# The rows of gate maxima and stabilisers, spread over the partitions by products or by reads from DRAM

## The chip, the cores and the metric

The kernel runs on one core of a Trainium2 chip. The metric is the device time of one execution in microseconds (us). The core has a matrix engine (TensorE, PE, with its weight loads as PEld), a vector engine (VectorE, DVE), an engine for functions (ScalarE, ACT), a general engine (GpSimd, POOL), and a sequencer for transfers (SyncE, SP). Working memory is SBUF with 128 partitions; PE writes its results to PSUM, which is divided into eight banks of 128 x 512 floats. Inputs, outputs and the `sums` tiles lie in DRAM; sixteen DMA engines carry the transfers between DRAM and SBUF.

## The reference

One layer of a hybrid encoder block at 512 positions and width 1024: RMSNorm, one input projection into 10240 columns, a Fourier branch, an mLSTM branch with four heads of width 512, sigmoid gates that merge the two, an output projection, a residual and a final norm. The change touches the gates of the mLSTM branch only. Per head and direction:

```
bcum = jnp.cumsum(ft, axis=-1)
dmat = bcum[..., :, None] - bcum[..., None, :] + it[..., None, :]
m_t = jnp.maximum(bcum + m_st[..., None], jnp.max(dmat, axis=-1))
s_mat = jnp.einsum('bhtd,bhsd->bhts', qt, kt) * jnp.exp(dmat - m_t[..., None])
...
h_out = num / jnp.maximum(jnp.abs(den), jnp.exp(-m_t))[..., None]
```

`ft` is the logarithm of the forget gate, `it` the input gate. The kernel computes this for all 512 positions at once instead of chunk by chunk. With `a = it - bcum` and `mx` the running maximum of `a`, the weight of source position s for target t is exp(a[s] - mx[t]), and the stabiliser is m[t] = bcum[t] + mx[t]. The weights are held as tiles with s in the partitions and t along the row; so `a` is needed as a column (one value per partition), but `mx` and `m` are needed as rows that stand in all partitions.

## The kernel before

All large products run in single-precision `float32r` form, split in two: a high part (`hi_of`, an ACT copy to `float32r`) and a low part (`lo_of`, a DVE subtraction), and three products per pair (`mm3`). Weights come as units of 512 KB (`fetch`, SP, into three buffers named `raw`); `prepare` splits a unit into `whi`/`wlo` (two buffers) and issues the next fetch; `unit` hands out a split unit and keeps the next one ready. At certain counts `unit`, and twice per head the head's own code, call `next_job`: SP copies a 1 MB weight block from DRAM to DRAM (`sum`, L159) and POOL's queue adds another block onto an earlier one (L163). These sums are used much later, behind the four heads.

The order is partly written by hand. The framework's planner orders the instructions of each engine with a timing model when the program is built; what it chose is then fixed, and each engine issues in that order. `pin` ties an instruction to its place behind the one before it on the same engine or queue. All of the kernel's transfers that SP issues in the heads are pinned, so SP keeps the order of the program, and an instruction on SP that waits holds all those behind it.

Ahead of the heads lie the projections of the conv channels, the convolution, the product that gives the gates (`gate_mm`, L302), and two z units. Then four heads run (`for h in range(NH)`, L474). In a head:

- q is projected (`mm3` at L498); in head 0 `gate_chain` (L420) follows, which makes the rows for all heads and both directions at once: biased gates (L433, L434), log-sigmoid, scans on DVE (L443, L447), and copies that put the backward rows into forward order (L451, L452). The results are `an` (for `a`), `mxn` (for `mx`) and `mn` (for `m`), 64 x 512 tiles; row 32 dr + h belongs to direction dr and head h. `gate_cols` (L459) transposes `an` to columns `a_col`.
- `mx_r` and `em_r` (L453 to L455) hold the rows of `mxn` and `mn` as high parts in partitions 0 to 63 and low parts in 64 to 127. `bsel` (L456) holds selector columns.
- `decay` (L512): per direction one product (L516) with a selector column as stationary side puts row h of `mx` into all partitions of a PSUM bank; eight exponentials (L521) read it and write the weight tiles `wf`; POOL clears the triangles (L525, L528).
- The products q k (L539, banks `sps`) are multiplied with the weights on DVE (L576, L577), summed over source blocks (L589 to L593), split (L605, L606) and summed over partitions by products with `half_r` (L608) into `den`: partitions 0 to 63 hold the forward sum, the others the backward sum.
- One product (L602) with `bw` (L601), made from `bsel`, puts `m` of the forward direction into partitions 0 to 63 of the bank `bc` and that of the backward direction into the others. `em` = exp(-bc) (L610); then the maximum with |den|, the reciprocal (L613, L614), and the scaling of the weights (L623 to L625), their split, the products v (L636), and the products with v (L651).
- The o products (`o_part`, L557 to L559) and z units are put between these steps as work for PE. In head 0 the last z unit runs ahead of `gate_cols` and `decay`; o units 0 and 1 and three pieces of unit 2 stand ahead of L608.

Of the kernel before, what the change touches and what calls it, by code (L numbers as in the profile page):

```python
# [40 lines left out]
def hybrid_block(ctx: ExitStack, tc, xT, xn, first, units, blocks, vecs, gates, gbias, consts, dft, fnw, out):  # L41
# [23 lines left out]
    def tl(tag, shape, dtype=F32, bufs=1, pool=None, shift=0):  # L65
        count[0] += 1
        if pool is None:
            pool = "wide" if tag[:2] in ("sa", "sb") else "gw" if tag in ("gwh", "gwl") else "low" if tag in LOW else "high" if tag in HIGH else "work"


        n = math.prod(shape[1:])
        t = pools[pool][1].tile([shape[0], -(-(n + shift) // 64) * 64], dtype, tag=tag, name=f"{tag}_{count[0]}", bufs=bufs)
        t = t[:, shift : shift + n]
        if len(shape) == 2:
            return t
        names = "abcd"[: len(shape) - 1]
        return t.rearrange(f"p ({' '.join(names)}) -> p {' '.join(names)}", **dict(zip(names, shape[1:])))
# [8 lines left out]
    def pin(ins, on=True):  # L86
        return tc.keep_in_program_order(ins) if on else ins
# [325 lines left out]
            gate_mm(pending[::-1])  # L413

    a_col = tl("a_col", [P, 4, 64])
    em_r = tl("em_r", [P, S], F32R)
    mx_r = tl("mx_r", [P, S], F32R)
    bsel = tl("bsel", [P, 8], F32R)

    def gate_chain():  # L420

        gb = tl("gb", [64, 2])
        pin(nc.sync.dma_start(gb, gbias))
        graw = t2k()
        se.activation(graw, gate_ps, AF.Copy)
        spare = [tl(t, [64, 2, S]) for t in ("so0", "so1")]
        s0, s1, s2, s3 = spare[0][:, 0, :], spare[0][:, 1, :], spare[1][:, 0, :], spare[1][:, 1, :]
        s4, s5 = tl("wf2", [64, S]), tl("wf3", [64, S])
        ig, z, e, u, w = s0, s1, s2, s3, s4
        for j, t in enumerate((ig, z)):  # L430
            sp = bank("acc", rows=64)
            te.matmul(sp, ident_c[:, C_SEL + 64 * j : C_SEL + 64 * j + 64], graw, start=True, stop=True)
            se.activation(t[0:32, :], sp[0:32, :], AF.Identity, bias=gb[0:32, j : j + 1])  # L433
            se.activation(t[32:64, ::-1], sp[32:64, :], AF.Identity, bias=gb[32:64, j : j + 1])  # L434
        se.activation(e, z, AF.Abs)
        se.activation(e, e, AF.Exp, scale=-1.0)
        ve.tensor_scalar(out=u, in0=e, scalar1=1.0, scalar2=None, op0=ALU.add)
        ve.scalar_tensor_tensor(out=w, in0=u, scalar=-1.0, in1=e, op0=ALU.add, op1=ALU.subtract)
        se.activation(u, u, AF.Ln)
        ve.scalar_tensor_tensor(out=w, in0=z, scalar=0.0, in1=w, op0=ALU.min, op1=ALU.add)  # L440
        ve.tensor_tensor(out=w, in0=w, in1=u, op=ALU.subtract)
        fc = e
        ve.tensor_tensor_scan(out=fc, data0=ones[0:64, 0:1].to_broadcast([64, S]), data1=w, initial=0.0,  # L443
                              op0=ALU.mult, op1=ALU.add)
        a, mx = u, z
        ve.tensor_tensor(out=a, in0=ig, in1=fc, op=ALU.subtract)
        ve.tensor_tensor_scan(out=mx, data0=a, data1=a, initial=0.0, op0=ALU.max, op1=ALU.max)  # L447
        ve.tensor_tensor(out=fc, in0=fc, in1=mx, op=ALU.add)
        an, mxn, mn = s5, s0, s4
        for dst, srct in ((an, a), (mxn, mx), (mn, fc)):  # L450
            ve.tensor_copy(dst[0:32, :], srct[0:32, :])  # L451
            ve.tensor_copy(dst[32:64, ::-1], srct[32:64, :])  # L452
        for dst, srct in ((mx_r, mxn), (em_r, mn)):  # L453
            se.activation(dst[0:64, :], srct, AF.Copy)
            ve.tensor_tensor(out=dst[64:128, :], in0=srct, in1=dst[0:64, :].bitcast(F32), op=ALU.subtract)  # L455
        pin(se.activation(bsel, ident_c[:, C_BSEL : C_BSEL + 8], AF.Copy))  # L456
        return an

    def gate_cols(an):  # L459
# [14 lines left out]
    for h in range(NH):  # L474
# [37 lines left out]
        def decay():  # L512
            ws = [tl(f"wf{b}", [P, 640]) for b in range(4)]
            for dr in range(2):
                bc = bank("acc")
                te.matmul(bc, bsel[:, 4 * dr + h : 4 * dr + h + 1].to_broadcast([P, P]), mx_r, start=True, stop=True)  # L516
                for b in range(4):
                    n = (b + 1) * P
                    o, s = (slice(n, 640), slice(b * P, S)) if dr == 0 else (slice(0, n), slice(0, n))
                    r = 32 * dr + h  # L520
                    se.activation(ws[b][:, o], bc[:, s], AF.Exp, scale=-1.0, bias=a_col[:, b, r : r + 1])  # L521
            for b in range(4):
                n = (b + 1) * P
                blk = ws[b][:, n : n + P]
                gp.affine_select(out=blk, in_=blk, compare_op=ALU.is_ge, fill=0.0, base=0,  # L525
                                 pattern=[[1, P]], channel_multiplier=-1)
                blk = ws[b][:, n - P : n]
                gp.affine_select(out=blk, in_=blk, compare_op=ALU.is_ge, fill=0.0, base=0,  # L528
                                 pattern=[[-1, P]], channel_multiplier=1)
            return ws  # L530
# [64 lines left out]
        early = 3 if h == 0 else 0  # L595
        w2 = unit()
        o_part(2, w2, PIECES[:early])
        em, bc, den = tl("phi2", [P, S]), bank("wk"), bank("wk")
        halves = [slice(0, 64), slice(64, 128)]
        bw = tl("plo2", [P, 2, 64], F32R)  # L600
        se.activation(bw, bsel.bitcast(F32).rearrange("p (r i) -> p r i", r=2)[:, :, h : h + 1].to_broadcast([P, 2, 64]), AF.Copy)  # L601
        te.matmul(bc, bw.rearrange("p r m -> p (r m)"), em_r, start=True, stop=True)  # L602
        for dr, acc in enumerate((sf, sb_)):
            sh, sl = tl(f"vhi{3 - dr}", [P, S], F32R), tl(f"vlo{3 - dr}", [P, S], F32R)
            hi_of(sh, acc)  # L605
# [1 line left out]
            for part, rr in enumerate((sh, sl)):  # L607
                te.matmul(den, half_r[:, dr, :], rr,  # L608
                          start=dr == 0 and part == 0, stop=dr == 1 and part == 1)
        se.activation(em, bc, AF.Exp, scale=-1.0)  # L610
        r = t2k()
        se.activation(r, den, AF.Abs)
        ve.tensor_tensor(out=r, in0=r, in1=em, op=ALU.max)  # L613
# [45 lines left out]
        for d in range(4):  # L659
            if h > 0 and d > 0:  # L660
                z_unit(d)
            c = c0 + d
            se.activation(xc[c], xc[c], AF.Copy, scale=col(V_SK + c))
        for d in range(4):
            c = c0 + d
            tp = bank("wk")
            for t in range(4):
                te.transpose(tp[:, t * P : (t + 1) * P], so[t][:, d * P : (d + 1) * P], ident)  # L668
            uu = t2k()
            ve.scalar_tensor_tensor(out=uu, in0=tp, scalar=col(V_HN + c), in1=xc[c], op0=ALU.mult, op1=ALU.add)  # L670
            ve.tensor_tensor(out=uu, in0=uu, in1=sz[d], op=ALU.mult)
            u_hi[c] = tl(f"sa{c}", [P, S], F32R)
            u_lo[c] = tl(f"sb{c}", [P, S], F32R)
            hi_of(u_hi[c], uu)
            lo_of(u_lo[c], uu, u_hi[c])
# [482 lines left out]
```

## Time and profile before

| | |
|---|---|
| median of three runs | 758.74 us (758.71 to 758.91) |
| the profiled execution | 758.77 us |
| its span in the trace | 756.8 us |
| mean granted clock of PE | 0.997 |
| PE busy | 747.5 us, 4134 products |
| DVE, ACT, POOL busy | 526.7, 411.8, 69.7 us |
| moved by DMA | 128.55 MB, 170 GB/s mean |

The profiled execution's own time is two microseconds above the span, which runs from the first to the last instruction of the program. Rows of a timeline give start and length in us, the engine, the line of the kernel, the operation, what it writes and reads, and shapes; a bracket at the end tells how long the engine sat idle before it and for whom. "SPq" rows are transfers issued by SP; their length is the issue, and the transfers themselves land later. In rows of the DMA view the last number is the median time from issue to landing. A product's length includes its way through the array; the next product starts before it ends.

### The profile page before, as it was taken

The page shows a single profiled execution, that of the slowest core. Times are in us where ns is not written, and L with a number is a line of the kernel's source. Part 1 is how long each engine was busy: PE and PEld are TensorE (multiplying, and loading weights), DVE is VectorE, ACT ScalarE, POOL GpSimd, SP SyncE. Part 2 cuts the span into 40 slices and gives each one's busy share as a digit, 9 for nine tenths or more (in the row PEclk, how much of TensorE's full clock was granted, in tenths as well). Part 3 has the DMA queues.
Part 4 walks back from the last instruction along what each step waited for, and adds up shares of the span by engine and source line. Part 5 has one row for each costly group of instructions (what it writes and reads, how often), then busy time and mean ns, then how long its engine had stood idle before and what let it go on. Part 6 is the DMA issues. An engine that isn't in the chain of part 4 may idle for free.

```text
span 756.8 us, 10920 instructions
## 1 busy us (share of the span) xinstructions
PE 747.5 (99%) x4134; PEld 642.3 (85%) x4134; DVE 526.7 (70%) x821; ACT 411.8 (54%) x645; POOL 69.7 (9%) x147
## 2 busy tenths in 40 slices
PE   9999999999999999999999999999999999999996
PEld 7888876888888888888888888899999999988885
DVE  6999983696658575867493856257676687556976
ACT  7336466478547663776372443266544587543444
POOL 0000000104100310041003010000020100000003
PEclk9999999999999999999999999999999999999998
DMA  8548775276924892479215873377655456554452
GB/s 301 168 141 227 209 256 141 48 244 150 225 101 156 212 241 69 162 180 228 100 59 166 221 228 106 88 216 213 190 162 163 114 163 197 171 182 153 139 195 111
DMA packets 40805, 128.55 MB, mean 170 GB/s; under 512 B 4785, under 2 KB 5426, under 8 KB 35634
## 3 DMA queue, kind: packets, MB, share of 16 engines
q1 hardware_dynamic: 36802, 104.41, 41.4%
q0 software_dynamic: 3520, 23.07, 15.3%
q8 instruction: 32, 0.52, 0.3%
q10 hardware_dynamic: 432, 0.40, 0.2%
q14 instruction: 19, 0.16, 0.1%
HBM read 125.76 MB, written 44.04 MB: 224 GB/s over the span
## 4 chain that ended last, share of the span: by engine, by line
PE 96%; DVE 1%; ACT 1%; DMA 0%; POOL 0%; issue 0%; POOLq 0%; ACTq 0%
PE acc L97 17%; PE acc L99 17%; PE acc L98 17%; PE wk L97 8%; PE wk L99 8%; PE wk L98 8%; PE acc L558 3%; PE acc L557 3%; PE acc L559 3%; PE wk L636 2%; PE acc L1006 1%; PE acc L1008 1%; PE acc L1007 1%; PE wk L302 1%; PE wk L668 1%; PE wk L608 1%
## 5 line engine op out<-in xcount | busy, mean ns | idle before, releaser
L93 DVE TENSOR_TENSOR wlo<-raw,whi 128x1024 fp32r<-128x1024 f32 (+2 forms) x107 | 124.9, 1171 | 79.0 <-ACT whi L90 78.6
L90 ACT ACTIVATE whi<-raw 128x1024 fp32r<-128x1024 f32 (+2 forms) x107 | 108.6, 1019 | 126.3 <-PE acc L98 76.5
L97 PE MATMUL acc<-hhi,whi 128*128 128x512 f32 x240 | 94.3, 393 | 0.6 <-ACT whi L90 0.6
L98 PE MATMUL acc<-hlo,whi 128*128 128x512 f32 x240 | 93.6, 390 | 0.0
L99 PE MATMUL acc<-hhi,wlo 128*128 128x512 f32 x240 | 93.5, 390 | 0.0
L93 DVE TENSOR_TENSOR gwl<-raw,gwh 128x1024 fp32r<-128x1024 f32 (+1 forms) x39 | 47.1, 1208 | 16.9 <-ACT gwh L90 16.9
L90 ACT ACTIVATE gwh<-raw 128x1024 fp32r<-128x1024 f32 (+1 forms) x39 | 40.9, 1048 | 29.0 <-PE acc L98 10.0
L97 PEld LDWEIGHTS acc<-hhi,whi 128*128 128x128 f32 x240 | 45.1, 188 | 11.1 <-ACT whi L90 1.2
L99 PEld LDWEIGHTS acc<-hhi,wlo 128*128 128x128 f32 x240 | 45.0, 188 | 9.5
L98 PEld LDWEIGHTS acc<-hlo,whi 128*128 128x128 f32 x240 | 45.1, 188 | 9.1
L559 PE MATMUL acc<-whi,hlo 128*128 128x512 f32 x128 | 50.4, 394 | 0.0
L558 PE MATMUL acc<-wlo,hhi 128*128 128x512 f32 x128 | 50.4, 394 | 0.0
L98 PE MATMUL acc<-sb,whi 128*128 128x512 f32 x128 | 50.1, 391 | 0.0
L97 PE MATMUL acc<-sa,whi 128*128 128x512 f32 x128 | 49.8, 389 | 0.0
L98 PE MATMUL wk<-vlo,phi 128*128 128x512 f32 x128 | 49.8, 389 | 0.0
L97 PE MATMUL wk<-vhi,phi 128*128 128x512 f32 x128 | 49.6, 389 | 0.0
L99 PE MATMUL acc<-sa,wlo 128*128 128x512 f32 x128 | 49.0, 391 | 0.0
L99 PE MATMUL wk<-vhi,plo 128*128 128x512 f32 x128 | 48.0, 389 | 0.0
L557 PE MATMUL acc<-whi,hhi 128*128 128x512 f32 x128 | 47.7, 393 | 0.0
L331 DVE SCALAR_TENSOR_TENSOR t2k<-sa,vecs,t2k 128x511 f32<-128x511 f32 (+1 forms) x64 | 45.1, 743 | 0.1
L93 DVE TENSOR_TENSOR vlo<-wk,vhi 128x512 fp32r<-128x512 f32 x32 | 20.6, 676 | 15.7 <-ACT vhi L90 15.7
L98 PEld LDWEIGHTS acc<-sb,whi 128*128 128x128 f32 x128 | 24.0, 188 | 5.0
(409 smaller groups left out, 1910.8 us busy)
## 6 DMA issues: line engine op xcount, KB each, us to landing
raw<-in_units_dram SPq DMA_DIRECT2D x69, 512.0 KB, 4.2
sum<-in_blocks_dram SPq DMA_DIRECT2D x20, 1024.0 KB, 8.0
raw<-sum SPq DMA_DIRECT2D x64, 256.0 KB, 3.6
raw<-in_blocks_dram SPq DMA_DIRECT2D x48, 256.0 KB, 3.8
sum<-in_blocks_dram POOLq DMA_DIRECT2D x10, 1024.0 KB, 10.6
sum<-sum POOLq DMA_DIRECT2D x10, 1024.0 KB, 8.6
raw<-sum SPq DMA_DIRECT2D x8, 512.0 KB, 4.2
raw<-in_blocks_dram SPq DMA_DIRECT2D x6, 512.0 KB, 4.1
```

Of the source, the lines that this page charges most:

```text
L90: pin(se.activation(dst, src, AF.Copy, scale=scale), pinned)
L93: pin(ve.tensor_tensor(out=dst, in0=src, in1=hi.bitcast(F32), op=ALU.subtract), pinned)
L97: pin(te.matmul(acc, wh, xh, start=start, stop=False, **skip), pinned)
L98: te.matmul(acc, wh, xl, start=False, stop=False, **skip)
L99: te.matmul(acc, wl, xh, start=False, stop=stop, **skip)
L302: pin(te.matmul(gate_ps[rows, :], w_gate[j][:, i, :], r, start=n == 0, stop=n == 14, tile_position=(0, 32 * (2 * b + j))), n + b + j > 0)
L331: ve.scalar_tensor_tensor(out=cv[:, o], in0=src[:, s], scalar=cw[k], in1=cv[:, o], op0=ALU.mult, op1=ALU.add)
L557: te.matmul(ops[t], hv(x_hi, k)[:, ts], wh[:, ks], start=k == 0, stop=False)
L558: te.matmul(ops[t], hv(x_hi, k)[:, ts], wl[:, ks], start=False, stop=False)
L559: te.matmul(ops[t], hv(x_lo, k)[:, ts], wh[:, ks], start=False, stop=k == 7)
L608: te.matmul(den, half_r[:, dr, :], rr, start=dr == 0 and part == 0, stop=dr == 1 and part == 1)
L636: te.matmul(vp[:, ds], xm[c0 + d][:, b * P : (b + 1) * P], vbf[:, d, :], start=True, stop=True)
```

## The change

The products that spread rows (L516 and L602) and what feeds them (`mx_r`, `em_r` as split tiles, `bsel`, `bw`) go. `mxn` and `mn` are written to two DRAM tiles of 64 x 512 (`rows0`, `rows1`) by SP, and `spread_rows(h)` reads them back for one head: row 32 dr + h of `mx` into all 128 partitions, once per direction (256 KB each), and the two rows of `m` into 64 partitions each of one tile `em` (128 KB each). The tiles have one buffer, so a read waits until the head before has used them. The reads for head 0 are issued at the end of the gate chain, those for head h + 1 near the end of head h, after its z units; all are pinned, as are both writes. The copies to forward order are put in another order: `mxn` first, then `an`, then `mn`. The exponentials then read SBUF, and `em` is computed in place.

```diff
+    kept_rows = [dram.tile([64, S], F32, tag=f"rows{j}", name=f"rows{j}") for j in range(2)]
+    spread = {}
+
+    def spread_rows(h):
+        for dr in range(2):
+            r = 32 * dr + h
+            spread[dr] = tl(("mx_r", "em_r")[dr], [P, S])
+            pin(nc.sync.dma_start(spread[dr], kept_rows[0][r : r + 1, :].to_broadcast([P, S])))
+        spread[2] = tl("em", [P, S])
+        for dr in range(2):
+            r = 32 * dr + h
+            pin(nc.sync.dma_start(spread[2][64 * dr : 64 * dr + 64], kept_rows[1][r : r + 1, :].to_broadcast([64, S])))
...
-        for dst, srct in ((an, a), (mxn, mx), (mn, fc)):
-            ve.tensor_copy(dst[0:32, :], srct[0:32, :])
+        for n, (dst, srct) in enumerate(((mxn, mx), (an, a), (mn, fc))):
+            pin(ve.tensor_copy(dst[0:32, :], srct[0:32, :]), n > 0)
             ve.tensor_copy(dst[32:64, ::-1], srct[32:64, :])
-        for dst, srct in ((mx_r, mxn), (em_r, mn)):
-            se.activation(dst[0:64, :], srct, AF.Copy)
-            ve.tensor_tensor(out=dst[64:128, :], in0=srct, in1=dst[0:64, :].bitcast(F32), op=ALU.subtract)
-        pin(se.activation(bsel, ident_c[:, C_BSEL : C_BSEL + 8], AF.Copy))
+            if n != 1:
+                pin(nc.sync.dma_start(kept_rows[n // 2], dst))
+        spread_rows(0)
         return an
...
             for dr in range(2):
-                bc = bank("acc")
-                te.matmul(bc, bsel[:, 4 * dr + h : 4 * dr + h + 1].to_broadcast([P, P]), mx_r, start=True, stop=True)
+                bc = spread[dr]
...
-        em, bc, den = tl("phi2", [P, S]), bank("wk"), bank("wk")
+        em, den = spread[2], bank("wk")
         halves = [slice(0, 64), slice(64, 128)]
-        bw = tl("plo2", [P, 2, 64], F32R)
-        se.activation(bw, bsel.bitcast(F32).rearrange("p (r i) -> p r i", r=2)[:, :, h : h + 1].to_broadcast([P, 2, 64]), AF.Copy)
-        te.matmul(bc, bw.rearrange("p r m -> p (r m)"), em_r, start=True, stop=True)
...
-        se.activation(em, bc, AF.Exp, scale=-1.0)
+        se.activation(em, em, AF.Exp, scale=-1.0)
...
+        if h < NH - 1:
+            spread_rows(h + 1)
         for d in range(4):
             c = c0 + d
             tp = bank("wk")
```

More of the change, by code (lines that the diff above doesn't have):

```diff
@@ L415, in hybrid_block @@
     a_col = tl("a_col", [P, 4, 64])
-    em_r = tl("em_r", [P, S], F32R)
-    mx_r = tl("mx_r", [P, S], F32R)
-    bsel = tl("bsel", [P, 8], F32R)
+    kept_rows = [dram.tile([64, S], F32, tag=f"rows{j}", name=f"rows{j}") for j in range(2)]
[9 more added lines that the diff above has]
+            pin(nc.sync.dma_start(spread[2][64 * dr : 64 * dr + 64], kept_rows[1][r : r + 1, :].to_broadcast([64, S])))
     def gate_chain():
```

## The prediction

> **What bounds the kernel.** I read the page first (busy shares, then the chain that ended last), next the waits of TensorE (PE), then PE's timeline around the products that the change removes, and last the timelines of ACT, DVE and SyncE (SP) around the gate chain of head 0. Of the page:
>
> ```profile
> span 756.8 us, 10920 instructions
> ...
> PE 747.5 (99%) x4134; PEld 642.3 (85%) x4134; DVE 526.7 (70%) x821; ACT 411.8 (54%) x645; POOL 69.7 (9%) x147
> ...
> GB/s 301 168 141 227 209 256 141 48 244 150 225 101 156 212 241 69 162 180 228 100 59 166 221 228 106 88 216 213 190 162 163 114 163 197 171 182 153 139 195 111
> ...
> PE 96%; DVE 1%; ACT 1%; DMA 0%; POOL 0%; issue 0%; POOLq 0%; ACTq 0%
> ```
>
> PE is busy 747.5 of 756.8 us and holds 96% of the chain. "Busy" alone could hide gaps, since products overlap; so I also read PE's waits (who was waited for, total us, times, longest):
>
> ```profile
> PE wk L196 <- POOL mhalf L183: 1.1, 1, 1.1
> PE acc L97 <- ACT whi L90: 0.6, 1, 0.6
> PE wk L608 <- ACT vhi L90: 0.4, 1, 0.4
> ```
>
> Three waits, 2.1 us in all, 1.1 of them at the very start. So PE sets the time nearly everywhere, and a product taken away is worth the distance from its start to the start of the next one, if no new wait takes its place. These distances stand in PE's timeline (start, us, engine, line); the last two rows are pieces of the chain of waits:
>
> ```profile
> 140.24 0.74 PE L516 MATMUL acc<-mx_r,bsel 128*128 128x512 f32 x2
> 140.81 0.40 PE L557 MATMUL acc<-whi,hhi 128*128 128x512 f32 x1
> ...
> 151.72 0.39 PE L602 MATMUL wk<-em_r,plo 128*128 128x512 f32 x1
> 152.55 0.50 PE L608 MATMUL wk<-vhi,half_r 128*128 128x512 f32 x1 [0.45 <-ACT vhi L90]
> 152.89 1.72 PE L636 MATMUL wk<-mhi,sa 128*128 128x128 f32 x14
> ...
> 169.03 0.40 PE L516 MATMUL acc<-mx_r,bsel 128*128 128x512 f32 x1
> 169.26 0.39 PE L97 MATMUL wk<-vhi,phi 128*128 128x512 f32 x1
> ...
> 169.88 0.49 PE L516 MATMUL acc<-mx_r,bsel 128*128 128x512 f32 x1
> 170.22 0.40 PE L97 MATMUL wk<-vhi,phi 128*128 128x512 f32 x1
> ...
> 221.03 0.39 PE L602 MATMUL wk<-em_r,plo 128*128 128x512 f32 x1
> 221.26 0.39 PE L97 MATMUL acc<-hhi,whi 128*128 128x512 f32 x1
> ...
> 238.68 0.47 PE acc L516 x2
> ...
> 313.87 0.47 PE acc L516 x2
> ```
>
> The duration column (0.39) is not the price: the next product starts 0.23 us later.
>
> **What it removes from PE.** Twelve products: per head two at L516 and one at L602. Pairs of L516: head 0 0.57 (140.24 to 140.81), head 1 0.23 + 0.34, heads 2 and 3 0.47 each: 2.08 us. L602: 0.23 in each of four heads (221.03 to 221.26; in head 0 the rest of its 0.83 is the wait of L608): 0.92 us. Sum 3.0 us.
>
> **What of it is real time.** Heads 1 to 3 hold 2.2 us of it, with PE gapless before and after: real. In head 0 it is 0.57 + 0.23 = 0.80, and there PE already waits for ACT at L608. That chain runs from the last z product over ACT's exponentials and DVE's products to L608, and the removed products are not on it; so PE would only come 0.8 us sooner to the same wait. What can fill it is L636: 14 of these products (the v of this head) run right behind L608 at 152.89, and they need neither removed operand. One PSUM bank (`bc` at L598) also becomes free for them. The planner issues what is ready, so I take them as moved ahead: the 0.8 is real, and the 0.45 of wait may go too. If not, head 0 gives nothing.
>
> **What it takes from ACT and DVE.**
>
> ```profile
> 136.03 0.63 ACT L454 ACTIVATE mx_r<-so 64x512 fp32r<-64x512 f32 x1 [6.21 <-DVE so L452]
> ...
> 137.67 0.31 ACT L601 ACTIVATE plo<-bsel 128x128 fp32r<-128x128 f32 x1
> ...
> 144.05 3.46 ACT L521 ACTIVATE wf<-acc,a_col 128x512 f32<-128x512 f32 x8
> ...
> 152.93 1.04 ACT L90 ACTIVATE whi<-raw 128x1024 fp32r<-128x1024 f32 x1
> ```
>
> ```profile
> 132.56 1.22 DVE L447 TENSOR_TENSOR_SCAN so<-so 64x512 f32<-64x512 f32 x1
> ...
> 135.58 0.42 DVE L452 COPY so<-so 32x512 f32<-32x512 f32 x1
> ...
> 136.91 0.69 DVE L455 TENSOR_TENSOR mx_r<-so,mx_r 64x512 fp32r<-64x512 f32 x1
> ```
>
> ACT loses two L454 (0.63 each), four L601 (0.31 each) and a tiny one at L456, some 2.7 us; DVE two L455, 1.4 us. Both engines have idle time (54% and 70% busy) and their results come well before PE needs them; I count zero. The exponentials now read SBUF instead of PSUM: the trace has ACT copies of 128x512 from both sides at about the same length, so zero again, bounded by PE's slack on both sides.
>
> **What it adds: the round trip in head 0.** The maxima are written to DRAM when their copies are done. Before, that is 135.58 + 0.42 = 136.0; the change puts these copies first, so up to 1.4 us sooner (the scan ends at 133.8). I keep 136.0. No row shows a write of gate rows or a read of one row into all partitions, so bounds come from the nearest DMAs (last number: median us to landing):
>
> ```profile
> yb<-in_xn_dram SPq DMA_DIRECT2D x8, 256.0 KB, 2.6
> out_dram<-yb SPq DMA_DIRECT2D x7, 256.0 KB, 2.3
> ...
> vlo<-in_xT_dram SPq DMA_DIRECT2D x4, 256.0 KB, 6.0
> ...
> gb<-in_gbias_dram SPq DMA_DIRECT2D x1, 0.5 KB, 7.3
> ```
>
> The write is like `out_dram<-yb` (SBUF to DRAM, 2.3; half its bytes), each read like `yb<-in_xn` (128 rows of 2 KB, 2.6); high, both like `vlo<-in_xT`, 6.0, which stood in a full queue. Near case: 136.0 + 2.3 + 2.6 = 140.9, the second read some 0.6 behind (SP's issue), 141.5. The exponentials start at 144.05, after a table load that follows the last z unit's SiLU: 2.5 us of cover, cost zero. High case: 136.0 + 6.0 + 6.0 = 148.0, 4 us late.
>
> The Trainium skill, page "DMA: Bandwidth & Descriptors", section "Latency and other measured facts", speaks against this read: it reports that partition streams running in step at a large power-of-two row pitch fall to about 103 GB/s, and guesses that they hit the same HBM channel. A read of one row by all partitions has pitch zero, so it may be the extreme of that; by 103 GB/s (an estimate from that page) a read takes about 2.5 us of transfer, the second would land near 145, the first near 143. By it the sum stays as it is and only the cover shrinks (the second direction's exponentials start half-way through L521's 3.46 us). No row of before shows such a read.
>
> **What it adds: SP's queue.** SP issues in the order of the program. The write stands behind `gb` and ahead of a block copy and the next fetches:
>
> ```profile
> 104.18 0.59 SPq L423 DMA_DIRECT2D gb<-in_gbias_dram  x1
> 104.81 0.65 SPq L159 DMA_DIRECT2D sum<-in_blocks_dram  x1
> ...
> 108.77 5.58 SPq L131 DMA_DIRECT2D raw<-in_units_dram  x2
> 114.41 0.50 SPq L159 DMA_DIRECT2D sum<-in_blocks_dram  x1
> ...
> 156.39 0.33 SPq L131 DMA_DIRECT2D raw<-in_units_dram  x1
> ...
> 237.43 0.33 SPq L131 DMA_DIRECT2D raw<-in_units_dram  x1
> ...
> 312.08 0.33 SPq L131 DMA_DIRECT2D raw<-in_units_dram  x1
> ```
>
> So a copy of 1 MB, two weight fetches and one more copy, issued at 104.8 to 114.4, wait behind SP's instruction until the maxima are written (about 138.3), then behind the four reads, to about 141. This is a large shift, 27 to 32 us, and its cover must be named: the two fetches (units for o products 2 and 3) are split by ACT only from 152.93 on. Ahead of the first lie 0.75 MB of reads, 1 MB of copy and its own 0.5 MB: at 250 to 300 GB/s (the page's busy slices) 7.5 to 9 us from 138.3, so 146 to 147.5; the second 2 us later. Five and four us of cover; cost zero. If one came after 152.93, PE would wait for it one to one. The copies feed block sums used after 400 us; POOL's add behind the first copy is issued behind head 0's masks, so it holds nobody.
>
> **Heads 1 to 3.** The reads are issued behind the fetches at 156.39, 237.43 and 312.08. L521 of head 1 cannot start before 169.03, 12 us later. For head 2 and 3:
>
> ```profile
> 243.49 2.62 ACT L521 ACTIVATE wf<-acc,a_col 128x512 f32<-128x512 f32 x6
> ...
> 323.30 1.42 ACT L521 ACTIVATE wf<-acc,a_col 128x512 f32<-128x512 f32 x3
> ```
>
> Head 2 has 243.49 - 237.8 = 5.7 us for two reads behind a 512 KB fetch: near 3 + 0.6 + 0.5 us, high 6 + 0.6; at worst one us late, with L608 of that head 60 us away, so zero. Head 3 has 11 us. The added 0.75 MB per head (3 us of queue) delays fetches that have more than 10 us of cover. Zero.
>
> **Sum.** 758.77 (the profiled execution; its span of 756.8 and 2.0 around it) - 3.0 = 755.8. The median of the runs is 758.74, so the forecast is the same against it.
>
> **Rivals.**
> - Head 0 gives nothing: L608 stays tied to ACT and DVE, and nothing fills. For it: the 0.45 of wait that is there already; against: 14 L636 products ready behind it. 758.77 - 2.2 = 756.6.
> - Slower: the round trip ends after the table load of head 0. L521, the masks, DVE's products and L608 then all move by the delay, and PE waits since its order is fixed when the program is built. It decides once the delay is over 2.2 us, that is the first read landing after 146.3. At the high bound, 4.0 late: 758.77 - 2.2 + 4.0 = 760.6. For it: a read of one row 128 times is in no row; the `gb` row shows 0.5 KB taking 7.3 us behind a copy. Against: SP's queue holds nothing else at that time, just because all else waits behind the write.
> - The change does not do what it says: PE's total falls by 3 us, but the planner, with new times for SP, orders PE differently and puts back as much in waits for fetched units or in switches between kinds of products (0.33 instead of 0.23 us at 169.88). About 758.5. For it: four us of cover on a fetch shifted by 30; against: 2.1 us of waits in the whole kernel before, so the planner does this well.
>
> **Numbers.** What a measurement of this kernel can tell from no change is about 0.2%, 1.5 us: faster is under 757.2, slower over 760.3. Forecast 755.8: 0.50 (it reaches down to 754.7, if the two later waits, 1.0 us, go too). Head 0 gives nothing, 756.6: 0.20. Order puts it back, 758.5: 0.16. Slower, 760.6 and beyond, 0.14. Faster 0.70, same 0.16, slower 0.14. Range 754.7 to 760.6, which leaves out only the worse half of the slower case; the likeliest alone is 754.7 to 756.3.
>
> **What would show it.** PE has 4122 products, and its waits stay near 2 us. The two writes land within 3 us and the reads by 142; L521 of head 0 still starts near 144, L608 near 152.5 with L636 ahead of it. SP issues nothing between `gb` and about 135, and the split that was at 152.93 doesn't wait for its fetch. I am wrong if PE shows a new wait in head 0 for L521's chain or for a `whi`, or if PE's waits grow elsewhere by as much as was removed.

## The result and the profile after

| | before | after |
|---|---|---|
| median | 758.73 us | 772.24 us (770.57 to 773.03, 4 runs) |
| span of the profiled execution | 756.8 us | 769.8 us |
| products on PE | 4134 | 4122 |

The changed kernel is slower: ratio 1.0171, interval 1.0158 to 1.0184. The forecast was 755.8, so it missed by 16 us, in sign too. (Ratios here and below are formed from the runs themselves, so they differ a little from the quotient of two medians.)

The page of the kernel after, the lines that answer to those of before:

```profile
span 769.8 us, 10907 instructions
PE 749.7 (97%) x4122; PEld 641.1 (83%) x4122; DVE 525.5 (68%) x819; ACT 405.2 (53%) x635; POOL 68.9 (9%) x147
PE 88%; ACT 4%; DVE 3%; DMA 2%; issue 1%; POOL 0%; SPq 0%; POOLq 0%; ACTq 0%
```

The twelve products are gone (4122), and yet PE is busy 2.2 us longer, and its share of the chain fell from 96% to 88%. Both need an answer. PE's waits, again as engine, tile, line, who was waited for, total us, times, longest:

```profile
PE acc L565 <- ACT whi L90: 4.2, 1, 4.2
PE acc L565 <- ACT so L580: 2.6, 2, 1.5
PE acc L566 <- DVE wlo L93: 2.1, 2, 1.2
PE acc L97 <- ACT whi L90: 1.9, 4, 0.7
PE wk L196 <- POOL mhalf L183: 1.1, 1, 1.1
PE acc L99 <- DVE wlo L93: 1.1, 2, 0.5
```

Waits of 13.0 us instead of 2.1, the longest for a split weight (`whi`) that has nothing to do with the gates. (In every kernel here PE's busy time and its waits add up to the span less 7.1 to 7.4 us, so a loss stands in one or the other.) ACT's timeline says why that split was late (start, us, engine, line, then what ACT was idle for). In this kernel L615 is the exponential of `em`, L369 the SiLU of z, L529 the exponentials of the weights:

```profile
146.02 1.28 ACT L615 ACT_TABLE_LOAD   x1 [16.03 <-DMA em<-rows]
147.32 0.63 ACT L615 ACTIVATE em<-em 128x512 f32<-128x512 f32 x1
147.85 1.04 ACT L90 ACTIVATE whi<-raw 128x1024 fp32r<-128x1024 f32 x1
148.91 1.28 ACT L369 ACT_TABLE_LOAD   x1
...
150.85 1.28 ACT L529 ACT_TABLE_LOAD   x1
152.15 1.92 ACT L529 ACTIVATE wf<-mx_r,a_col 128x512 f32<-128x512 f32 x4
```

ACT stood still for 16 us until the rows of `m` had come back from DRAM, and only then did the split (139.73 before), the SiLU and the exponentials (144.05 before, 152.15 now). Nothing needs `em` before the maximum with |den|, which DVE starts at 156.88 in the kernel before and at 167.83 here. But the planner had put L615 at the head of that row, behind the logarithm of the gate chain, and ACT issues in its fixed order. L615 stands early in the later heads too: at 172.61, 252.98 and 332.53, where the kernel before has it at 221.5, 302.5 and 377.2. In head 1 ACT idles 3.69 us for it, and PE waits twice soon after (near 175 and 178, the row of 2.6 us above).

The writes and the reads of the maxima went about as forecast. SP's timeline, and the DMA view of the stretch 135.8 to 142.5 (last number: us from issue to landing):

```profile
138.15 0.34 SPq L424 DMA_DIRECT2D mx_r<-rows  x1
138.55 0.45 SPq L424 DMA_DIRECT2D em_r<-rows  x1
139.35 1.11 SPq L428 DMA_DIRECT2D em<-rows  x2
```

```profile
raw<-in_units_dram SPq DMA_DIRECT2D x2, 512.0 KB, 8.6
mx_r<-rows SPq DMA_DIRECT2D x1, 256.0 KB, 3.6
em_r<-rows SPq DMA_DIRECT2D x1, 256.0 KB, 5.2
em<-rows SPq DMA_DIRECT2D x2, 128.0 KB, 6.0
rows<-so SPq DMA_DIRECT2D x1, 128.0 KB, 2.2
```

The maxima were in SBUF at 138.15 + 3.6 = 141.8 and 138.55 + 5.2 = 143.8, both ahead of 144.05. What came later, 6 us behind its issue, was `em`, whose time the forecast had never looked at.

That PE is busy longer with less work has its own reason. A view by stretches gives the granted clock (PEclk) beside PE's busy time and count of products:

```profile
144.40:148.90 4.50, 0.37 (x2) 0.00 (x0) 0.00 (x0) 2.86 (x3) 0.00 (x0) 1.00 1.00 400
150.00:153.40 3.40, 3.40 (x10) 2.62 (x9) 0.15 (x1) 3.36 (x6) 0.29 (x1) 0.50 0.96 394
153.40:156.80 3.40, 3.40 (x16) 2.81 (x15) 2.05 (x5) 3.40 (x7) 2.62 (x8) 1.00 0.08 34
```

After the gap of some 4.2 us PE ran at full clock for 1.1 us and then for 3.4 us at half of it: 10 products in the time of 16, about 1.5 us on top of the gap (an estimate: six products at 0.23 us). Without the twelve products PE's busy time should have come to 745.4 us (the two memset kernels below have that), so 4.3 us have to be explained; the clock explains 1.5, the nine more waits about 0.16 us each (a product ahead of a wait counts with its whole 0.39 us), and the rest stays open.

### The profile page after: what moved, and what is told of

Read it like the earlier page. It is cut to its first block, busy times and chain, and to the rows that moved or that the text cites. A ratio compares the mean times of both kernels' runs of the same rounds, so it can differ in the third digit from the quotient of the medians.

```text
span 769.8 us, 10907 instructions
## 1 busy us (share of the span) xinstructions
PE 749.7 (97%) x4122; PEld 641.1 (83%) x4122; DVE 525.5 (68%) x819; ACT 405.2 (53%) x635; POOL 68.9 (9%) x147
## 4 chain that ended last, share of the span: by engine, by line
PE 88%; ACT 4%; DVE 3%; DMA 2%; issue 1%; POOL 0%; SPq 0%; POOLq 0%; ACTq 0%
PE acc L97 17%; PE acc L99 16%; PE acc L98 16%; PE wk L99 7%; PE wk L97 7%; PE wk L98 7%; PE acc L566 3%; PE acc L567 3%; PE acc L565 3%; DMA em<-rows 2%; PE wk L641 1%; PE acc L1015 1%; PE acc L1014 1%; PE acc L1013 1%; PE wk L302 1%
## 5 line engine op out<-in xcount | busy, mean ns | idle before, releaser
L99 PE MATMUL acc<-hhi,wlo 128*128 128x512 f32 x240 | 93.4, 389 | 0.0
L99 PEld LDWEIGHTS acc<-hhi,wlo 128*128 128x128 f32 x240 | 45.1, 188 | 9.4
L99 PE MATMUL acc<-sa,wlo 128*128 128x512 f32 x128 | 49.0, 392 | 1.1 <-DVE wlo L93 1.1
L99 PE MATMUL wk<-vhi,plo 128*128 128x512 f32 x128 | 48.5, 389 | 0.0
L565 PEld LDWEIGHTS acc<-whi,hhi 128*128 128x128 f32 x128 | 24.2, 190 | 13.2 <-ACT whi L90 4.9
```

What stands on the lines that cost most here:

```text
L99: te.matmul(acc, wl, xh, start=False, stop=stop, **skip)
L565: te.matmul(ops[t], hv(x_hi, k)[:, ts], wh[:, ks], start=k == 0, stop=False)
```

## The experiments

Fourteen kernels ran; times are medians of 4 to 11 runs, the kernel before beside them gave 758.75 to 758.89. The intervals reach some 0.1%, 0.8 us, to each side, so smaller differences between two kernels are not told apart.

| run | what it is | us | ratio, interval |
|---|---|---|---|
| em_pinned | after, L615 held in its place | 761.80 | 1.0047, 1.0034 to 1.0059 |
| mx_read | only the maxima by DRAM | 763.58 | 1.0054, 1.0040 to 1.0068 |
| m_read | only `m` by DRAM | 769.71 | 1.0143, 1.0129 to 1.0157 |
| no_spread | no products, no transfers | 761.79 | 1.0039, 1.0026 to 1.0052 |
| banks_first | em_pinned, two banks held in head 0 | 761.55 | 1.0038, 1.0026 to 1.0051 |
| banks_all | the same in all heads | 759.90 | 1.0017, 1.0008 to 1.0026 |
| order_first | em_pinned, o unit 2 behind `den` in head 0 | 759.92 | 1.0023, 1.0013 to 1.0033 |
| no_spread_banks | no_spread, banks held in head 0 | 761.00 | 1.0035, 1.0022 to 1.0047 |
| before_freed | before, banks freed early by DVE copies | 761.31 | 1.0033, 1.0021 to 1.0044 |
| combo | order_first and banks held in heads 1 to 3 | 759.79 | 1.0011, 1.0002 to 1.0020 |
| banks_memset | banks_all, held by DVE instead of PE | 759.99 | 1.0015, 1.0006 to 1.0024 |
| combo_memset | combo, held by DVE instead of PE | 760.50 | 1.0021, 1.0012 to 1.0030 |
| no_em | before without L602 | 760.25 | 1.0018, 1.0009 to 1.0026 |
| twice | before, the twelve products issued twice | 761.53 | 1.0037, 1.0023 to 1.0050 |

### Where the large loss comes from: em_pinned, mx_read, m_read, no_spread

The first theory: the large loss is the place of L615 on ACT, not the round trip. **em_pinned** ties L615 to its place in the program and changes nothing else:

```diff
-        se.activation(em, em, AF.Exp, scale=-1.0)
+        pin(se.activation(em, em, AF.Exp, scale=-1.0))
```

> The changed kernel, with the exponential of the stabiliser (L615) tied to its place behind the split of the two sums, so that it can't stand early on ACT. Theory H (the exponential waits for the last of the reads, and all of ACT behind it waits too): the split that waited until 147.9 starts near 140, the exponentials of the weights near 144 to 145, PE's wait of 4.6 us at 144.4 is gone, and with twelve products less the time is 755.5 to 757.5 us. Rival R (SP held from 104 to 141, so weight fetches and reads land late): PE still waits in head 0, 766 us or more. Rival O (the planner's other order costs it in many places): 763 to 769.

ACT's timeline in em_pinned:

```profile
139.65 1.06 ACT L90 ACTIVATE whi<-raw 128x1024 fp32r<-128x1024 f32 x1 [9.89 <-PE acc L98]
...
143.96 1.92 ACT L529 ACTIVATE wf<-mx_r,a_col 128x512 f32<-128x512 f32 x4
...
149.60 1.06 ACT L90 ACTIVATE whi<-raw 128x1024 fp32r<-128x1024 f32 x1 [1.90 <-DMA raw<-in_units_dram]
...
155.44 0.61 ACT L615 ACTIVATE em<-em 128x512 f32<-128x512 f32 x1
```

The first split and the exponentials are back at the times of before (139.73, 144.05), L615 stands at 155. The median fell by 10.4 us (772.24 to 761.80; by the ratios 9.4, by the spans 10.1). That part is settled. But 3 us above before remain, with all twelve products gone, and theory H, which gave 755.5 to 757.5, missed by that much.

**mx_read** reads only the maxima back and keeps the product L602; **m_read** reads only `m` and keeps L516.

> Half of the change: only the maxima go through DRAM (one write, two reads per head); the stabiliser is spread by the product at L602 as before. H: no exponential stands early on ACT, eight products less at 2.1 us: 756 to 757.5 us. R: SP is held just as long and the fetches wait as before: 766 or more. O: 760 to 768.

> The other half: only the stabiliser goes through DRAM (one write, two reads of 64 partitions per head); the maxima are spread by products at L516 as before. H: its exponential stands early on ACT and waits for the reads, here with less ahead of them in the queue, to about 142; ACT's split and the weights' exponentials come 3 to 5 us late, four products less give 0.9 back: 760 to 764 us. R: SP is held as long, 766 or more. O: about 760.

m_read, in which the exponential of `em` (L617 there) again reads a tile that a transfer fills, has the large loss (769.71), with a wait of 3.6 us for a split among PE's waits; mx_read hasn't. Both carry the smaller one. m_read lies above the 760 to 764 of its theory and inside the range of the rival R. ACT's rows speak for H all the same: ACT idles 6.55 us for `em`, the split behind it starts at 144.72 and the weights' exponentials at 149.01, 5.0 us late as expected, and no fetch is waited for there. What H had left out: ACT idles 6.25 us more for `em` at 168.07 in head 1, and PE's clock is halved for 3.4 us twice. The 763.58 of mx_read holds such a stretch too; its two runs with a mean clock of 0.998 (the others 0.994 to 0.996) took 761.87 and 762.41.

**no_spread** takes the transfers away too. It is the kernel before without products, `bsel` and `bw`; the exponentials read the unspread rows, and `a_col` is multiplied by zero:

```diff
-                bc = bank("acc")
-                te.matmul(bc, bsel[:, 4 * dr + h : 4 * dr + h + 1].to_broadcast([P, P]), mx_r, start=True, stop=True)
+                bc = mx_r.bitcast(F32)
...
-        te.matmul(bc, bw.rearrange("p r m -> p (r m)"), em_r, start=True, stop=True)
...
-        se.activation(em, bc, AF.Exp, scale=-1.0)
+        se.activation(em, em_r.bitcast(F32), AF.Exp, scale=-1.0)
```

> The kernel before without the twelve spreading products and without any transfer in their place: the exponentials read the rows where they lie (so the weights are not the reference's), a_col is multiplied by zero so that all stays finite, and the rest runs as before. It prices the products alone. By the sum of the prediction: 755.8 us (3.0 less). If PE's time in head 0 turns into a wait: 756.6. If these products cost nothing: 758.7.

It takes 761.79, as long as em_pinned (761.80), with `den` at nearly the same places (156.3 and 392.2). So, as far as these two can tell, the writes, reads, and the shift of SP's queue cost nothing once L615 is in its place; and to take twelve products away, with no transfer put in their stead, makes this kernel 3 us slower, which none of the three cases expected (755.8, 756.6, 758.7). The two kernels differ in more than the transfers: no_spread keeps the split rows, and its exponential of `em` is not pinned. In head 0 that one stands early again, at 139.56 instead of 154.8, but its rows are there by then and ACT's split comes only 0.4 us later (140.10 instead of 139.73). So the early place in head 0 is there in every kernel whose exponential needs no product and is not pinned (after, m_read, no_spread, no_spread_banks, and no_em below); it is the wait for the transfer that makes it dear.

### What the smaller loss is: banks and the order on PE

PE's waits in em_pinned:

```profile
PE acc L97 <- ACT whi L90: 1.8, 4, 0.7
PE acc L565 <- ACT so L580: 1.7, 1, 1.7
PE acc L99 <- DVE wlo L93: 1.1, 2, 0.5
PE wk L196 <- POOL mhalf L183: 1.1, 1, 1.1
```

5.7 us instead of 2.1, of which one (1.7, near 168 us) is in head 0, five (2.6 in all) lie behind head 3 and two at the very start. (A wait costs some 0.16 us more than its row says, since it is counted from the end of a product of 0.39 us, whose successor could have started at 0.23.) The order on PE had changed. The rows show where `den` stands (first and last start of its products with the high part; before, em_pinned, before_freed, in this order; the view by source line):

```profile
L608 PE MATMUL wk<-vhi,half_r x8: 389/394/499, 152.6 to 380.4; 128*128 128x512 f32 x8
```

```profile
L613 PE MATMUL wk<-vhi,half_r x8: 389/392/476, 156.2 to 392.4; 128*128 128x512 f32 x8
```

```profile
L611 PE MATMUL wk<-vhi,half_r x8: 389/390/395, 156.5 to 391.4; 128*128 128x512 f32 x8
```

In head 0 it stands 3.6 us later, in head 3 12 us: work that is there to fill PE's time while a head's chain goes over ACT and DVE runs ahead of the chain instead. In head 0 these are o products (70 stand ahead of `den` instead of 48), in heads 1 to 3, where all o products stood ahead of it before, products of the projections (42 to 53 more) and in head 3 some of the next stage. At the end of head 3 this work is used up. Before, transposes of the last head (L668) and products of the next stage (`sa`) lie among each other; in em_pinned the transposes stand alone, with a wait behind them. Before, then em_pinned, PE's timeline:

```profile
414.91 0.40 PE L97 MATMUL acc<-sa,whi 128*128 128x512 f32 x1
415.14 0.38 PE L668 MATMUL wk<-consts,so 128*128 128x128 f32 x2
415.28 0.48 PE L98 MATMUL acc<-sb,whi 128*128 128x512 f32 x1
```

```profile
419.58 2.00 PE L675 MATMUL wk<-consts,so 128*128 128x128 f32 x12
422.29 0.50 PE L97 MATMUL acc<-sa,whi 128*128 128x512 f32 x1 [0.71 <-ACT whi L90]
```

The theory: of the four PSUM banks with the name `acc`, the two `bc` banks of L516 were taken until the last exponential, so o unit 0 could fill only two at a time; freed, all four go to filler, which runs ahead. The rival: the cause lies elsewhere (reading SBUF, the products themselves). **banks_first** holds two banks in head 0 by a product of one column and a copy of 128x1 behind the exponentials, **banks_all** in all four heads (its edit of em_pinned; banks_first has the same lines under `if h == 0`):

```diff
                 bc = spread[dr]
+                hold = bank("acc")
+                te.matmul(hold[:, 0:1], ident, a_col[:, 0, 0:1], start=True, stop=True)
...
+                pin(se.activation(tl("drain", [P, 1]), hold[:, 0:1], AF.Copy))
```

> em_pinned, and in head 0 two PSUM banks are held through the weights' exponentials, as the spreading products held them: a product of one column into each, read by a 128x1 copy on ACT behind the last exponential of its direction. Theory B (without the held banks all four o banks are free at once, PE finishes o unit 0 sooner, unit 2 is split before the two sums and its 24 products run ahead of L613, so den comes 3.7 us later and the cover behind it is gone): split of unit 2 back behind 151, L613 near 152.5, the wait near 168 gone, 756 to 757.5 us. Rival P (the planner's order scatters with any edit): 759 to 763. Rival D (the reads themselves slow PE down): stays at 761 to 762.

> The same in all four heads. B, with head 0 alone to blame: as banks_first within 1 us. If the banks matter in heads 1 to 3 too (the waits at 421 to 452): banks_first keeps 1 to 3 us of loss that this one hasn't. P: 759 to 763.

**order_first** leaves the banks alone and pins the rest of o unit 2 behind `den` in head 0:

```diff
-                te.matmul(ops[t], hv(x_hi, k)[:, ts], wh[:, ks], start=k == 0, stop=False)
+                pin(te.matmul(ops[t], hv(x_hi, k)[:, ts], wh[:, ks], start=k == 0, stop=False), pinned)
...
-        o_part(2, w2, PIECES[early:])
+        o_part(2, w2, PIECES[early:], h == 0)
```

> em_pinned with no bank held; in head 0 alone the products of o unit 2 behind its first three pieces are tied behind L613 (each piece's first product pinned to the one before it). If it is the place of o unit 2 that costs (B's second half): L613 at 152.5 to 154, 756.5 to 758.5 us. If the loss comes from elsewhere: 761 to 762.

**no_spread_banks** is no_spread with the banks held in head 0.

> no_spread (no spreading products, no transfers, rows read unspread, a_col times zero) with the two banks held in head 0 as in banks_first. B: 755.5 to 757, the 3.0 us of the products back, and the difference to banks_first is what the transfers cost. P: anywhere from 757 to 763.

Held in head 0 alone the banks bring little (761.80 to 761.55; 761.79 to 761.00), though `den` of head 0 is back at 152.9 and the wait near 168 is down to 0.3 us in banks_first: theory B, which gave 756 to 757.5 for that, failed. Held in all heads, or with the order pinned in head 0, the kernel comes to 759.9, and with the banks held `den` of head 3 is back near its old place (383.5; before 380.4, em_pinned 392.4). In order_first it isn't (391.2), and the time is the same; so the place of `den` alone does not tell the time. The waits of banks_all:

```profile
PE wk L196 <- POOL mhalf L183: 1.1, 1, 1.1
PE acc L526 <- DVE a_col L472: 0.8, 1, 0.8
PE acc L99 <- DVE wlo L93: 0.5, 1, 0.5
PE acc L97 <- ACT whi L90: 0.3, 1, 0.3
PE acc L526 <- ACT so L583: 0.3, 1, 0.3
```

3.0 us, and of these 1.1 (both rows of L526) belong to the dummy products themselves.

**before_freed** is the reverse test: the kernel before with all its products, but DVE copies each `bc` to SBUF, so that its bank comes free ahead of the exponentials.

```diff
                 te.matmul(bc, bsel[:, 4 * dr + h : 4 * dr + h + 1].to_broadcast([P, P]), mx_r, start=True, stop=True)
+                bs_ = tl(f"bcs{dr}", [P, S])
+                ve.tensor_copy(bs_, bc)
+                bc = bs_
```

> The kernel before with all its products; only each bank bc of L516 is copied to SBUF by DVE (128x512, some 0.6 us each, DVE is 70% busy) and the exponentials read the copy, so that the two banks come free before the exponentials instead of behind them. Theory (freed banks let filler run ahead of the chain of head 0 and of the later heads): it loses what em_pinned loses beside its twelve products, 3.0 + 3.0 = 6 us less whatever 0.3 us the products cost beside it: 763 to 765.5, den's products of head 0 near 156 to 157 instead of 152.6, and new waits for weight splits at 420 to 455 of about 3 us in all. Rival (the loss of em_pinned comes from the removed products or from reading SBUF, not from the banks): within 0.2% of before, 757.5 to 760.2, no new late waits.

It takes 761.31: slower than before, though by 2.4 us and not by the 4 to 7 that the theory gave. `den` stands within 1 us of where em_pinned has it (156.5 and 391.4, quoted above). So freed banks, with all products kept, change the order in that way, and it costs; what the eight copies on DVE cost by themselves was not run apart (DVE is busy 4.0 us longer). The late waits are 1.3 us, not the 3 expected: of the 2.7 us in the span, 0.6 are waits and 1.9 are PE's busy time (749.4 instead of 747.5). The 2.4 us are less than half of the 3.0 + 3.0 us that separate em_pinned from the forecast.

### Is there a version that gains?

**combo** puts order_first and the held banks of heads 1 to 3 together.

> em_pinned with both mends that worked alone: in head 0 the rest of o unit 2 is pinned behind den (as in order_first), in heads 1 to 3 two PSUM banks are held through the exponentials (as in banks_all). Theory (two separate losses of some 2 us in head 0 and 3 us at the end): the two gains add up: 761.8 - 1.9 - 2.0 to 2.5 = 757.4 to 758.2, with the wait near 168 gone and the late waits under 1 us, thus no slower than before, 758.76. Rival (one loss seen twice, the distance by which filler runs ahead): no better than either alone, 759.5 to 760.3, with late waits of some 2 us left.

759.79: the gains of 1.9 us each did not add up. By the distances between the starts the six dummies took 1.9 us of PE here and the eight of banks_all 1.5 (not the 2.5 that the expectation below puts on them), so **banks_memset** and **combo_memset** hold the banks by a DVE memset of 128x1.

> banks_all with one thing changed: the two banks per head are taken by a DVE memset of 128x1 instead of a product of one column, so PE issues 4122 products. In combo the 6 dummies cost PE 1.88 us, so 8 cost 2.5 in banks_all. Theory (with the order of before back, the removed products are worth their distances): 759.9 - 2.5 = 757.4, range 756.9 to 758.2, below before (758.8); den's products near 153, 229, 306, 383 and waits under 3 us in all. Rival (whatever PE saves, waits for splits take it back, since the splits on ACT and DVE set the pace of the later heads): 759.0 to 760.2, with the late waits at 420 to 452 back at 2 us or more.

> combo with the same change (memset instead of the one-column product in heads 1 to 3; in head 0 the pin). Theory: 759.8 - 1.9 = 757.9, range 757.3 to 758.6. Rival as for banks_memset: 759.0 to 760.2 with late waits of 2 us or more.

Neither gained: 759.99 and 760.50. PE's busy time fell to 745.4 us in both, 2.1 less than before. The waits of banks_memset:

```profile
PE wk L196 <- POOL mhalf L183: 1.1, 1, 1.1
PE acc L568 <- DVE sz L367: 1.0, 2, 0.6
PE acc L97 <- ACT whi L90: 1.0, 1, 1.0
PE wk L616 <- ACT vhi L90: 1.0, 1, 1.0
PE wk L97 <- ACT phi L90: 0.7, 1, 0.7
PE acc L99 <- DVE wlo L93: 0.5, 1, 0.5
```

5.3 us in seven waits, of six kinds: PE's busy time fell by 2.1 us against before and its waits grew by 3.2, three of the six kinds new. No one edit had aimed at these places.

### Is a product worth its distance at all? no_em and twice

**no_em** is the kernel before without L602 and its bank, the banks of L516 kept; **twice** issues each of the twelve products two times.

```diff
-        bw = tl("plo2", [P, 2, 64], F32R)
...
-        te.matmul(bc, bw.rearrange("p r m -> p (r m)"), em_r, start=True, stop=True)
...
-        se.activation(em, bc, AF.Exp, scale=-1.0)
+        se.activation(em, em_r.bitcast(F32), AF.Exp, scale=-1.0)
```

> The kernel before without L602, its stationary side (L601) and its bank; the exponential of em reads the unspread rows em_r, so em is not that of the reference; no transfer is added and the two banks of L516 stay. Theory A (a product is worth its distance as long as the banks hold the order): 758.8 - 0.7 to 0.9 = 757.9 to 758.1. Theory B (each edit of PE's work makes the planner order anew, and what it gains goes into waits): 758.6 to 760.0, with PE's waits up by as much as PE's busy time falls.

> The kernel before with each of its twelve spreading products (L516, L602) issued twice in a row into the same bank; nothing else. Theory A (worth its distance): 758.8 + 12 x 0.23 = 761.6, 761.2 to 762.2. Theory B (waits and order absorb or add): outside of that, either under 760.5, because the added products lie in time that was waited anyhow, or over 762.5, because the order gets worse.

Twelve products more cost 2.8 us (761.53; five runs, 761.52 to 762.09), 12 x 0.23: an added product costs its distance. Four products fewer cost 1.5 us (760.25) instead of bringing 0.9. PE's waits in no_em:

```profile
PE wk L196 <- POOL mhalf L183: 1.1, 1, 1.1
PE wk L605 <- ACT vhi L90: 0.9, 1, 0.9
PE acc L97 <- ACT whi L90: 0.6, 1, 0.6
PE acc L99 <- DVE wlo L93: 0.5, 1, 0.5
```

`den` of head 0 (L605 here) waits 0.9 us for its split instead of 0.4, so in head 0 the freed time turned into wait. Not all of that is the product's: the exponential of `em` stands early here too (139.47), and the split `vhi` starts 0.26 us later for it (152.13 instead of 151.87). So no_em does not price L602 alone. The wait at L99 is new. The rows explain 1.0 of the 1.4 + 0.9 us between its span (758.2) and the one forecast; the rest stands in PE's busy time (747.7 us, 0.2 more than before with four products fewer), which is not traced to one place.

## Why the prediction was wrong

**That PE sets the time, and 0.23 us per product: right for a product added.** `twice` measures it.

**The round trip in head 0, cost zero: right.** Writes landed in 2.2 us (2.3 foreseen), the maxima at 141.8 and 143.8 (140.9 and 141.5 foreseen, cover to 144.05, of which 0.2 us was left). The page "DMA: Bandwidth & Descriptors" of the Trainium skill, section "Latency and other measured facts", which the prediction had weighed against the change, gave 143 and 145 by its estimate: both reads landed 1.2 us sooner than by that rule, later than by the nearest rows. em_pinned, with the transfers, and no_spread, without them, have the same time within what their runs can tell (761.80 and 761.79).

**SP's queue, cost zero: right in the sum, not in the sizes.** The two fetches took 8.6 us from issue to landing (median of the two) and came at about 150 and 151, the first instead of 146 to 147.5, the second instead of some 2 us after that; in em_pinned the split that needs the first waited 1.90 us for it (the row at 149.60), still ahead of 152.93. And of the reads of heads 1 to 3 only those of the maxima went out behind the fetches; SP held those of `em`, and all behind them, until DVE was done with the one buffer of `em` (three times, 41.6 us in all):

```profile
SPq L428 <- DVE t2k L618: 41.6, 3, 21.5
```

The prediction had passed over that buffer. No run shows a price for it apart from L615: em_pinned has the same wait (45.4 us), and its time is that of no_spread.

**"ACT ... I count zero": the step that failed, 10 of the 16 us.** The prediction asked what an exponential costs that reads SBUF instead of PSUM, and not when it may run. Before, L610 depended on the product L602, which the planner placed close ahead of `den`; so its place on ACT was late (154.8). The change made it depend on a transfer alone. The planner put it ahead of three steps that PE's filler and the weights hang on, and the transfer took 6 us; ACT idled 16.03 us, and one pin took 10.4 us off. What times the planner reckoned with, no run shows; but in all five kernels in which this exponential needs no product and is not pinned, it stands early in head 0 (139.5 to 147.3). The doubt that the prediction stated for itself ("a new wait in head 0 ... for a whi") was the right place to look, reached by another cause than the one it priced.

**"A product taken away is worth the distance ..., if no new wait takes its place": the condition failed, 3.0 expected and 3.0 lost.** The prediction saw the freed bank of L602 and took it for a gain, and did not see that the two banks of L516 had been holding the filler back; before_freed puts 2.4 of these 6.0 us on them, the rest stays open. The rival "planner's other order" had the mechanism and a price 3.3 us too small: it gave 758.5, while em_pinned, the change without the early exponential, takes 761.8. It argued against itself that before had only 2.1 us of waits. That was the wrong way round: two of these three waits (1.1 and 0.6) stand in the first 6.1 us, ahead of all the heads, so a new order had 0.4 us of wait to win and much to lose. For the rival "head 0 gives nothing" no_em shows a like case (the wait of `den` grew from 0.4 to 0.9, half of it by the early exponential), but in the kernel after, and in em_pinned, `den` has another place, and the price of 756.6 came out nowhere.

**The rival that was slower** had the right chain (L521, the masks, DVE's products and L608 all came late, L521 at 152.15) but put the cause on the maxima, which landed in time. The delay came through `em`, which was read last and needed last.

**What stays open.** Freed banks, with the copies that free them, cost 2.4 us; held banks give 1.9 back. With banks held and no dummies 1.2 us remain above before, and taking away four products alone costs 1.5. The runs show that waits, and small distances in PE's busy time, come up at other places for each program, not why the planner's order is worse each time. No run was below the kernel before; the best, combo, is at 1.0011 (1.0002 to 1.0020).

## What to carry to other kernels

When an edit changes what an instruction waits for (a transfer instead of a product), look up where it may now stand on its engine: on an engine that issues in order, something not needed for 10 us can hold up all that is needed at once, and one `pin` was worth 10 us here. A buffer or bank that an edit frees is no gain by itself, since it may have been what held filler back for later. Where a planner orders the program anew and PE has almost no waits, price added products at their distance but removed ones at nothing, until the new order has been looked at.

## What the hardware showed unexpectedly

- PE's granted clock fell to 0.50 for 3.4 us after an idle stretch of 4.2 us; that is about 1.5 us more than the wait row shows. Less idle time can be enough: in mx_read two waits of 1.2 and 0.5 us, 1.7 us without work in 3.4, had the same effect (stretches as above: the length, then PE's busy time and products; PEclk is third from the end):

```profile
422.04:425.45 3.41, 1.67 (x7) 0.93 (x6) 2.00 (x3) 2.41 (x5) 3.22 (x6) 1.00 0.84 267
425.45:428.87 3.42, 3.42 (x10) 2.65 (x9) 3.39 (x7) 0.97 (x2) 0.37 (x1) 0.50 0.85 163
```

  In m_read a wait of 2.0 us in head 1 was followed by it too. The wait of 1.7 us near 168 in em_pinned was not, and neither were those of 1.1 and 1.5 us near 175 and 178 in the kernel after. So the idle time alone does not settle it, and what does, these runs do not show. The Trainium skill, page "TensorE: Matmul & The Clock Gate", section "Part 1: The HAM clock gate", says that an idle window of about 3.4 us halves the clock and as long a busy one restores it. The length of the halved stretch agrees (3.4 us); that PE must be idle for a whole window does not hold here, and the measured 1.7 us decide.
- Reads of one DRAM row into many partitions took 3.6 us from issue to landing for the first 256 KB, 5.2 for the second and 6.0 for the 128 KB behind them: each landed later behind its issue than the one ahead of it, though each is small.
